# A hybrid SSD and gated-MLP layer on one core: a convolution on zero-padded copies, and the matmuls of an SSD group in fewer places

## Chip, cores and metric

The kernel runs on 1 core of one Trainium2 chip. The metric is the device time of one execution in microseconds. Five engines work side by side: PE (TensorE, matmuls), DVE (VectorE), ACT (ScalarE), POOL (GpSimd) and SP, which here only issues DMAs. Each engine takes its instructions strictly in the order in which the program holds them.

## The reference, cut to what matters

One layer: 256 context tokens and 256 latent tokens, width 2048. The normed and modulated tokens go through one input projection; its first 4096 columns (32 tiles of 128 channels) get a depthwise convolution of five taps and a SiLU, and feed a bidirectional Mamba-2 scan (SSD) in 8 groups of 4 heads and chunks of 128 tokens.

```python
def _dwconv_rows(x, w, b, n_rows, row_len):
    xp = pad(x.reshape(bsz, n_rows, row_len, C), 2 zeros on both ends of each row)
    y = b
    for k in range(5):
        y = y + xp[:, :, k:k + row_len] * w[k]
xbc = silu(_dwconv_rows(z[..., :4096], conv_w, conv_b, n_rows, row_len))
# context: 1 row of 256; latent: 4 rows of 64
states = einsum('bckgn,bckgr,bckgrp->bcgrpn', Bc, decay_to_end, xdt)
CB = einsum('bcqgn,bckgn->bcgqk', Cc, Bc)
y_diag = einsum('bcgqk,bcgrqk,bckgrp->bcqgrp', CB, exp(masked differences of cumsum(dt*A)), xdt)
y_off = einsum('bcqgn,bcgrpn,bcqgr->bcqgrp', Cc, h_starts, exp(acs))
out = x + gate * rmsnorm(concat(rmsnorm((y + D*x) * silu(z_ssd)), gated_mlp) @ w_out)
```

## The kernel before, in words

Every large product runs on PE as three matmuls of split operands (`mm3`, lines 139 to 141: high times high, high times low, low times high). For that, ACT casts each half of a streamed weight tile (`hi_w`, line 80) and DVE subtracts (`lo_w`, line 81), some halves ahead of PE, in four buffers.

The program has stages. First the adaLN products and seven of the 32 channel tiles are made, k by k, with their order written by hand. Then comes the stage that the change touches, about 137 to 480 us: the other 25 channel tiles are projected one after the other into a PSUM tile `psx` of a pool with two banks (`acp`), 48 matmuls a tile (512 columns, or 256 for the eight tiles of the C matrix, which only the latent tokens need). Between them the work of the SSD is strewn in. After it come 16 blocks of latent columns (`pa`, lines 877 to 879), the output projection (`pm`, `pq`), and a tail of norms and stores.

The order in the SSD stage comes from `later` and `pump`: `plan_tile` (line 660) files each step of a tile or a group under a due time, counted in units of which a tile takes 8 x 1.3 (8 x 0.65 for a C tile), and `pump` issues what is due after every second k step. A scheduler may move instructions a little within that. Group g consists of tiles 4g to 4g+3: two of x, one of B, one of C. Its steps:

- `conv_silu` (line 433): ACT writes `acc` = bias + middle tap (line 439), straight from the PSUM tile; DVE adds the four other taps (line 452), each as two instructions, one over the context row (252 to 255 columns) and one over the four latent rows (4 x 62 or 4 x 63), since a tap must not run over a row's end; ACT makes the SiLU (line 455). Tiles 4, 5 and 7 are first copied from PSUM to SBUF (`z4`, `z5`, `z7`, in unused parts of `y`).
- `ssd_x`, `ssd_b`: PE transposes x and B (`ptx`, `ptb`), ACT copies them out; `ssd_w`: POOL weighs x (`xw`, `xl`).
- `ssd_cb` (line 615): `pcb`, C times B for both chunks, on PE; DVE masks it (`cbf`, `cbb`).
- `ssd_states` (line 596): `psc` and `psl` on PE; ACT copies, POOL scales (line 612), DVE adds (line 613): the start states `hs`.
- `ssd_y(g, c)`, for one chunk: POOL starts `M` (line 633), DVE adds four heads (636) and multiplies by the decays `E` (638); PE makes `pso` = C times `hs` (640); DVE scales it into `yo`, POOL adds it to `y`.
- `ssd_yd(g, c)`: `psy` = `M` times x on PE (line 655), DVE adds it to `y`.
- `plan_e`: the decays of the next group. POOL issues a DMA of rows (`R`, line 529), ACT adds the columns (581), DVE takes the minimum (583, into `E`), ACT the exponential (590). `E`, `M`, `R` and `hs` have one buffer each, so that a new `M` waits until `psy` has read the old one, and `R` is loaded anew when `E` has been taken from it.

Of the kernel before, what the change touches and what calls it, by code (L numbers as in the profile page):

```python
# [40 lines left out]
def tile_hybrid_ssd_mlp(  # L41
# [388 lines left out]

    done = {}

    def conv_silu(i, src):
        ch = ORDER[i]
        lat = ch >= 24
        n = 256 if lat else 512
        acc = cv2.tile([P, n], F32, tag="acc", name=f"acc{i}")
# [4 lines left out]
        src4 = src[:, l0 : l0 + 256].rearrange("p (r t) -> p r t", r=4)
        for k in (0, 1, 3, 4):
            s = k - 2
            parts = [(acc4, src4, 64)]
            if not lat:
                parts.append((acc[:, 0:256], src[:, 0:256], 256))
            for (a, z, w) in parts:
                o0, o1 = max(0, -s), w - max(0, s)
                ao = a[..., o0:o1]  # L450
                zi = z[..., o0 + s : o1 + s]
# [1 line left out]
        tag = "xs" if ch < 16 else ("bs" if ch < 24 else "cs")
        o = cv2.tile([P, n], F32, tag=tag, name=f"xbc{i}")
        nc.scalar.activation(o, acc, AF.Silu)
        done[i] = o
# [171 lines left out]
    def ssd_y(g, c):  # L628
        S = gs_[g]
        E, cbf, cbb, xk, ct, hs = S["E"], S["cbf"], S["cbb"], S["xk"], done[4 * g + 3], S["hs"]  # L630
        h4 = slice(4 * g, 4 * g + 4)
# [7 lines left out]
        pso = spt([P, 2, 256], f"pso{g}{c}")  # L639
        nc.tensor.matmul(pso, lhsT=ct[:, c * P : (c + 1) * P], rhs=hs[:, c], start=True, stop=True)  # L640
        yo = cv1.tile([P, 2, 256], F32, tag="yo", name=f"yo{g}{c}")
        nc.vector.tensor_tensor(yo.rearrange("p d (h q) -> p d h q", h=4), pso.rearrange("p d (h q) -> p d h q", h=4),
                                bc(eac[:, c, :, h4], 3, 64), op=ALU.mult)
        yg = y[:, c, g * 256 : (g + 1) * 256]
        nc.gpsimd.tensor_tensor(hp(yg), hp(xk[:, 2 + c, :]), bc(dsk[:, h4], 2, 64), op=ALU.mult)
        nc.gpsimd.tensor_tensor(yg, yg, yo[:, 0, :], op=ALU.add)
        nc.gpsimd.tensor_tensor(yg, yg, yo[:, 1, :], op=ALU.add)
        S["M", c] = M

    def ssd_yd(g, c):  # L650
# [1 line left out]
        M, xk = S["M", c], S["xk"]
        psy = spt([P, 256], f"psy{g}{c}")
        for h in range(4):
            nc.tensor.matmul(psy[:, h * 64 : (h + 1) * 64], lhsT=M[:, h, :],
                             rhs=xk[:, 2 + c, h * 64 : (h + 1) * 64], start=True, stop=True)
        yg = y[:, c, g * 256 : (g + 1) * 256]
        nc.vector.tensor_tensor(yg, yg, psy, op=ALU.add)
# [409 lines left out]
```

## Time and profile before

| | |
|---|---|
| runs | 1009.81, 1009.97, 1011.67 us; median 1009.97 |
| the profiled execution's own time | 1012.65 us |
| its span, first to last instruction | 1010.9 us |
| granted TensorE clock over the span | 0.99 |
| PE, DVE, ACT, POOL busy | 981.3, 624.5, 493.1, 120.7 us |
| matmuls of the SSD stage between their casts: lines 139 to 141 | 400 each of 382, 366 and 369 ns (pipelined, so these overlap) |

A row of the profile gives an instruction group's line in the kernel, its engine, the tiles it writes and reads, how often, and its time. "Idle before" is the time in which the engine stood still just ahead of it, with the instruction whose end released it. A matmul of split operands with 512 columns starts every 0.227 us, one with 256 every 0.12 us, whatever the length shown for it.

### The profile page before, as it was taken

Reading aid. Unit: us, or ns where it says so; the run is one execution under the profiler, and the core shown is the slowest. Engines: PE = TensorE matmul, PEld = TensorE weight load, DVE = VectorE, ACT = ScalarE, POOL = GpSimd, SP = SyncE. Lnnn points to the kernel's source line nnn. Section 1 sums busy time; section 2 is a strip of 40 time slices with the busy share of each in tenths; the row PEclk is TensorE's granted clock in tenths of the full one; section 3 lists DMA queues with packets and bytes.
Section 4 is the critical chain, followed back from the end, with each engine's and each line's share of the span. In section 5 each row is a group of like instructions: output and inputs, shape, how many; then the busy total and the mean of one; then the engine's idle time right before and its main releaser. Section 6 shows DMA issues by size and latency. Waiting matters only on the chain.

```text
span 1010.9 us, 14117 instructions
## 1 busy us (share of the span) xinstructions
PE 981.3 (97%) x5600; PEld 797.0 (79%) x5600; DVE 624.5 (62%) x947; ACT 493.1 (49%) x762; POOL 120.7 (12%) x166
## 2 busy tenths in 40 slices
PE   6899999989999999999999999999999999999996
PEld 2788887767888888787888888877888888888885
DVE  3544478876575676766567767666655554445636
ACT  3433359754745636353545343455465564346522
POOL 1000003552224233223000000000000000000000
PEclk9899999999999999999999999999999999999998
DMA  9999654133332323323887777685455555556722
GB/s 355 417 419 419 269 195 170 42 131 120 125 125 84 125 107 118 110 84 133 326 306 277 282 272 281 248 323 175 166 193 182 189 186 181 194 205 218 281 87 84
DMA packets 31218, 207.28 MB, mean 205 GB/s; under 512 B 3696, under 2 KB 3840, under 8 KB 7472
## 3 DMA queue, kind: packets, MB, share of 16 engines
q1 hardware_dynamic: 28224, 192.44, 50.7%
q0 software_dynamic: 2208, 12.73, 3.7%
q10 hardware_dynamic: 720, 1.20, 0.3%
q8 instruction: 44, 0.72, 0.3%
q14 instruction: 22, 0.18, 0.1%
HBM read 204.20 MB, written 2.16 MB: 204 GB/s over the span
## 4 chain that ended last, share of the span: by engine, by line
PE 75%; DMA 8%; DVE 6%; ACT 4%; issue 3%; POOL 2%; DVEq 0%; SPq 0%; ACTq 0%; POOLq 0%
PE psx L139 8%; PE psx L140 8%; PE psx L141 8%; PE pa L877 8%; PE pa L878 8%; PE pa L879 8%; DMA gate<-in_wada_dram 6%; PE psada L214 3%; PE pm L922 3%; PE pm L923 3%; PE pm L924 3%; DVE lo_w L81 2%; PE pq L923 2%; PE pq L922 2%; PE pq L924 2%
## 5 line engine op out<-in xcount | busy, mean ns | idle before, releaser
L81 DVE TENSOR_TENSOR lo_w<-w,hi_w 128x1024 fp32r<-128x1024 f32 x234 | 286.5, 1231 | 199.3 <-ACT hi_w L80 195.9
L80 ACT CAST hi_w<-w 128x1024 fp32r<-128x1024 f32 x234 | 246.0, 1052 | 293.1 <-PE pa L879 141.8
L877 PE MATMUL pa<-hi_w,hhi 128*128 128x512 f32 x512 | 202.4, 395 | 0.0
L879 PE MATMUL pa<-hi_w,hlo 128*128 128x512 f32 x512 | 199.5, 390 | 0.0
L878 PE MATMUL pa<-lo_w,hhi 128*128 128x512 f32 x512 | 199.4, 390 | 0.0
L139 PE MATMUL psx<-hhi,hi_w 128*128 128x512 f32 (+1 forms) x400 | 152.7, 382 | 1.3 <-DVE acc L452 1.3
L141 PE MATMUL psx<-hhi,lo_w 128*128 128x512 f32 (+1 forms) x400 | 147.4, 369 | 0.0
L140 PE MATMUL psx<-hlo,hi_w 128*128 128x512 f32 (+1 forms) x400 | 146.5, 366 | 0.0
L877 PEld LDWEIGHTS pa<-hi_w,hhi 128*128 128x128 f32 x512 | 96.2, 188 | 20.5 <-issue 1.4
L879 PEld LDWEIGHTS pa<-hi_w,hlo 128*128 128x128 f32 x512 | 96.1, 188 | 20.3
L878 PEld LDWEIGHTS pa<-lo_w,hhi 128*128 128x128 f32 x512 | 96.3, 188 | 19.1 <-issue 0.2
L139 PEld LDWEIGHTS psx<-hhi,hi_w 128*128 128x128 f32 x400 | 75.8, 190 | 14.5 <-issue 3.5
L452 DVE SCALAR_TENSOR_TENSOR acc<-psx,pc,acc 128x248 f32<-128x248 f32 (+1 forms) x204 | 84.1, 469 | 3.1 <-ACT acc L439 2.4
L141 PEld LDWEIGHTS psx<-hhi,lo_w 128*128 128x128 f32 x400 | 75.7, 189 | 12.7 <-issue 0.5
L140 PEld LDWEIGHTS psx<-hlo,hi_w 128*128 128x128 f32 x400 | 75.7, 189 | 12.3 <-issue 1.4
L738 DVE SCALAR_TENSOR_TENSOR junk<-gate,cb 128x2048 bf16<-128x2048 f32 x16 | 36.7, 2292 | 30.5 <-DMA gate<-in_wada_dram 30.4
L922 PE MATMUL pm<-hi_w,hhi 128*128 128x512 f32 x128 | 50.0, 390 | 0.0
L923 PE MATMUL pm<-lo_w,hhi 128*128 128x512 f32 x128 | 49.9, 390 | 0.0
L924 PE MATMUL pm<-hi_w,hlo 128*128 128x512 f32 x128 | 49.7, 389 | 0.0
L581 ACT ACTIVATE R<-R,y 128x128 f32<-128x128 f32 x128 | 40.1, 390 | 14.6 <-DMA R<-acs 14.5
L139 PE MATMUL psx<-hhi,hi_st 128*128 128x512 f32 (+1 forms) x112 | 40.9, 365 | 0.0
L140 PE MATMUL psx<-hlo,hi_st 128*128 128x512 f32 (+1 forms) x112 | 40.8, 364 | 0.0
(217 smaller groups left out, 1270.5 us busy)
## 6 DMA issues: line engine op xcount, KB each, us to landing
w<-in_wlat_dram SPq DMA_DIRECT2D x64, 1024.0 KB, 4.8
ada<-in_wada_dram SPq DMA_DIRECT2D x32, 1024.0 KB, 14.5
w<-in_wout_dram SPq DMA_DIRECT2D x32, 1024.0 KB, 4.7
w<-in_wxbc_dram SPq DMA_DIRECT2D x25, 1024.0 KB, 4.8
gate<-in_wada_dram SPq DMA_DIRECT2D x16, 1024.0 KB, 5.7
R<-acs POOLq DMA_DIRECT2D x8, 1024.0 KB, 5.4
wst<-in_wst_dram SPq DMA_DIRECT2D x16, 480.0 KB, 13.8
xT<-in_xch_dram SPq DMA_DIRECT2D x4, 1024.0 KB, 10.0
```

The lines of the kernel that those rows point to most:

```text
L80: nc.scalar.copy(hi, raw)
L81: nc.vector.tensor_tensor(lo, raw, hi.bitcast(F32), op=ALU.subtract)
L139: nc.tensor.matmul(ps, lhsT=whi, rhs=hhi[k][:, s], start=start, stop=False)
L140: nc.tensor.matmul(ps, lhsT=whi, rhs=hlo[k][:, s], start=False, stop=False)
L141: nc.tensor.matmul(ps, lhsT=wlo, rhs=hhi[k][:, s], start=False, stop=stop)
L452: nc.vector.scalar_tensor_tensor(ao, zi, cw[:, k : k + 1], ao, op0=ALU.mult, op1=ALU.add)
L877: nc.tensor.matmul(pa[tk], lhsT=hhi[k][:, t], rhs=whi[:, w], start=k == 0, stop=False)
L878: nc.tensor.matmul(pa[tk], lhsT=hhi[k][:, t], rhs=wlo[:, w], start=False, stop=False)
L879: nc.tensor.matmul(pa[tk], lhsT=hlo[k][:, t], rhs=whi[:, w], start=False, stop=k == KT - 1)
L922: nc.tensor.matmul(p, lhsT=yh[:, t], rhs=whi[:, w], start=j == 0, stop=False)
L923: nc.tensor.matmul(p, lhsT=yh[:, t], rhs=wlo[:, w], start=False, stop=False)
L924: nc.tensor.matmul(p, lhsT=yl[:, t], rhs=whi[:, w], start=False, stop=hf == 0 and j == 15)
```

## The change

Convolution: a tile with context and latent tokens is first copied into an SBUF tile of 524 columns, with two zeros ahead of and behind the 256 context tokens and every row of 64 latent tokens; ACT does it, in two copies out of PSUM, into one of two such tiles (`zp`), whose zeros POOL has written once. `z4` and `z5` get that form too, by two DVE copies each. ACT's first tap and DVE's four others then run over 520 columns at once, one instruction a tap. The SiLU writes the two parts back without the gaps, as two instructions. C tiles are computed in place in the output tile, but else as before.

SSD group: `ssd_y` is split. `ssd_m` makes `M` and writes the product back over `E`, so that `psy` reads `E` and `M` is free at once. `ssd_o` makes `pso` of both chunks, one behind the other; `ssd_yd` makes `psy` of both. `ssd_cb` is due with `ssd_states`, both `pso` at 13 (they were at 9 and 12.5), both `psy` at 17.5 (13 and 17.5), the next group's decays from 18 (13). `gate`, `ssq` and `rr` move into one small tile, `at` to other columns of `y`.

```diff
+    def pad_rows(z, c0):
+        return z[:, c0 : c0 + 264].rearrange("p (r q) -> p r q", q=66)[:, :, 0:64]
+    def pad_in(copy, z, src):
+        copy(z[:, 2:258], src[:, 0:256])
+        copy(pad_rows(z, 260), src[:, 256:512].rearrange("p (r q) -> p r q", q=64))
...
+    nc.gpsimd.memset(y0[:, 384 : 384 + 2 * ZP], 0.0)
...
-                nc.vector.tensor_copy((z4, z5)[i], psx[4 + i])
+                pad_in(nc.vector.tensor_copy, (z4, z5)[i], psx[4 + i])
...
+    zps = [cv1.tile([P, ZP], F32, name=f"zp{n}") for n in range(2)]
...
-        nc.scalar.activation(acc, src, AF.Identity, bias=pc[:, C_CB + i : C_CB + i + 1], scale=cw[:, 2:3])
...
-                nc.vector.scalar_tensor_tensor(ao, zi, cw[:, k : k + 1], ao, op0=ALU.mult, op1=ALU.add)
...
+            pad_in(nc.scalar.copy, z, src)
+        n = ZP - 4
+        a = acc[:, 0:n]
+        nc.scalar.activation(a, z[:, 2 : 2 + n], AF.Identity, bias=cb, scale=cw[:, 2:3])
         for k in (0, 1, 3, 4):
+            nc.vector.scalar_tensor_tensor(a, z[:, k : k + n], cw[:, k : k + 1], a, op0=ALU.mult, op1=ALU.add)
+        nc.scalar.activation(o[:, 0:256], acc[:, 0:256], AF.Silu)
+        nc.scalar.activation(o[:, 256:512].rearrange("p (r q) -> p r q", q=64), pad_rows(acc, 258), AF.Silu)
...
-        nc.vector.tensor_tensor(M, M, E[:, c], op=ALU.mult)
+        nc.vector.tensor_tensor(E[:, c], M, E[:, c], op=ALU.mult)
...
+        pso = [spt([P, 2, 256], f"pso{g}{c}") for c in range(2)]
+        for c in range(2):
+            nc.tensor.matmul(pso[c], lhsT=ct[:, c * P : (c + 1) * P], rhs=hs[:, c], start=True, stop=True)
...
-            later(d0 + 5, lambda: ssd_cb(g))
+            later(d0 + 6, lambda: ssd_cb(g))
             later(d0 + 6, lambda: ssd_states(g))
-            later(d0 + 9, lambda: ssd_y(g, 0))
-            later(d0 + 12.5, lambda: ssd_y(g, 1))
-            later(d0 + 13, lambda: ssd_yd(g, 0))
-            later(d0 + 17.5, lambda: ssd_yd(g, 1))
-            plan_e(d0 + 13, g + 1)
+            later(d0 + 9, lambda: ssd_m(g, 0))
+            later(d0 + 12, lambda: ssd_m(g, 1))
+            later(d0 + 13, lambda: ssd_o(g))
+            later(d0 + 17.5, lambda: ssd_yd(g))
+            plan_e(d0 + 18, g + 1)
```

How instructions move shows in the order in which the engines hold them. On PE, in group 1, from `psl` (the second part of the states) to the first `pso`, before; the rows left out are matmuls of the projection, 30 of 256 columns and 2 of 512 in all:

```order
L606 MATMUL psl_2171<-xl_2103,bk_2000 128x256 x2
L139 MATMUL psx_2126<-hhi_125,hi_w_1896 128x256
...
L141 MATMUL psx_2126<-hhi_134,lo_w_1960 128x256
L139 MATMUL psx_2231<-hhi_119,hi_w_2045 128x512
L140 MATMUL psx_2231<-hlo_135,hi_w_2045 128x512
L640 MATMUL pso_2224<-hs_2174,xbc_1764 128x512
```

The same place of the changed kernel; 30 matmuls of 256 columns, 18 of 512 and the transposes of one B tile stand between:

```order
L632 MATMUL psl_2162<-xl_2067,bk_1992 128x256 x2
L141 MATMUL psx_2117<-hhi_124,hi_w_1889 128x256
...
L143 MATMUL psx_2215<-hhi_121,lo_w_2022 128x512
L593 MATMUL ptb_2240<-ident,xbc_2128 128x128 x4
...
L143 MATMUL psx_2215<-hhi_123,lo_w_2022 128x512
L672 MATMUL pso_2259<-hs_2165,xbc_1760 128x512
L672 MATMUL pso_2260<-hs_2165,xbc_1760 128x512
```

Both `pso` now stand together, 16 projection matmuls and a transpose further behind the states than the first did. From `psl` to the first `pso` there are, before and now, in groups 0 to 7: 29 and 30, 32 and 48, 18 and 36, 18 and 30, 12 and 30 (groups 4 to 6), 9 and 27 projection matmuls.

On POOL, from the first `M` of group 0 on, before, with what each waits for:

```order
L633 TENSOR_TENSOR M_1944<-cbb_1910,dtt 128x512 [waits DMAHW2_49,DVE_49]
L612 TENSOR_TENSOR hs_1925<-hs_1925,ed 128x256 [waits Activation_49] x2
L633 TENSOR_TENSOR M_2007<-cbb_1910,dtt 128x512 [waits DVE_49,PE_49]
L646 TENSOR_TENSOR y<-y,yo_1953 128x256 [waits DVE_49,Pool_49]
L647 TENSOR_TENSOR y<-y,yo_1953 128x256 [waits Pool_49]
L556 TENSOR_TENSOR xw_2098<-xk_1981,ed 128x256 [waits Activation_49]
```

And in the changed kernel:

```order
L659 TENSOR_TENSOR M_1937<-cbb_1909,dtt 128x512 [waits DMAHW2_49,DVE_49]
L638 TENSOR_TENSOR hs_1918<-hs_1918,ed 128x256 [waits Activation_49] x2
L659 TENSOR_TENSOR M_1985<-cbb_1909,dtt 128x512 [waits DVE_49,Pool_49]
L680 TENSOR_TENSOR y<-y,yo_2003 128x256 [waits DVE_49]
L681 TENSOR_TENSOR y<-y,yo_2003 128x256 [waits Pool_49]
L582 TENSOR_TENSOR xw_2062<-xk_1966,ed 128x256 [waits Activation_49]
```

The order is the same here, but the second `M` waits for DVE alone and no longer for PE.

## Rows read from the trace of the kernel before

**Rows 1.** The page, first part: each engine's busy time, share and instructions.
```profile
PE 981.3 (97%) x5600; PEld 797.0 (79%) x5600; DVE 624.5 (62%) x947; ACT 493.1 (49%) x762; POOL 120.7 (12%) x166
```

**Rows 2.** Windows of the SSD stage: us, then PE, PEld, DVE, ACT, POOL busy; PEclk, DMA, GB/s.
```profile
200.00:240.00 40.00, 35.18 (x162) 26.73 (x161) 28.36 (x57) 24.60 (x52) 18.37 (x25) 0.96 0.35 132
...
sum 340.00, PE 331.12 PEld 267.60 DVE 240.45 ACT 184.43 POOL 112.55; mean PE 41.39 PEld 33.45 DVE 30.06 ACT 23.05 POOL 14.07
```

**Rows 3.** Waits of PE over the span: us in total, how many, the longest.
```profile
PE pso L640 <- DVE hs L613: 5.2, 4, 2.2
...
PE psx L139 <- DVE acc L452: 1.3, 1, 1.3
...
PE ptb L567 <- ACT xbc L455: 0.7, 1, 0.7
PE pcb L620 <- ACT xbc L455: 0.7, 1, 0.7
...
PE ptx L547 <- ACT xbc L455: 0.5, 1, 0.5
PE psy L655 <- DVE M L638: 0.3, 1, 0.3
```

**Rows 4.** Timeline of PE, groups 0 and 1: start, length, instruction, idle before.
```profile
175.71 1.88 PE L603 MATMUL psc<-xw,bk 128*128 128x512 f32 x4
...
186.30 1.13 PE L640 MATMUL pso<-hs,xbc 128*128 128x512 f32 x2 [1.22 <-DVE hs L613]
...
199.35 1.88 PE L603 MATMUL psc<-xw,bk 128*128 128x512 f32 x4
...
209.90 1.99 PE L640 MATMUL pso<-hs,xbc 128*128 128x512 f32 x2 [2.19 <-DVE hs L613]
...
213.40 0.41 PE L139 MATMUL psx<-hhi,hi_w 128*128 128x512 f32 x1
```

**Rows 5.** Timeline of PE around pcb, psc and psl, in group 2 and in group 4.
```profile
230.00 0.39 PE L141 MATMUL psx<-hhi,lo_w 128*128 128x512 f32 x1
...
233.48 0.40 PE L140 MATMUL psx<-hlo,hi_w 128*128 128x512 f32 x1
...
317.51 0.39 PE L141 MATMUL psx<-hhi,lo_w 128*128 128x512 f32 x1
...
318.42 0.40 PE L140 MATMUL psx<-hlo,hi_w 128*128 128x512 f32 x1
...
319.33 0.39 PE L141 MATMUL psx<-hhi,lo_w 128*128 128x512 f32 x1
...
322.37 0.40 PE L140 MATMUL psx<-hlo,hi_w 128*128 128x512 f32 x1
```

**Rows 6.** Timeline of DVE: taps from PSUM (psx) and from SBUF (y), and hs.
```profile
155.76 6.29 DVE L452 SCALAR_TENSOR_TENSOR acc<-psx,pc,acc 128x248 f32<-128x248 f32 x16
...
163.10 0.83 DVE L452 SCALAR_TENSOR_TENSOR acc<-y,pc,acc 128x248 f32<-128x248 f32 x1
...
177.72 7.86 DVE L452 SCALAR_TENSOR_TENSOR acc<-y,pc,acc 128x248 f32<-128x248 f32 x16
185.50 0.74 DVE L613 TENSOR_TENSOR hs<-psl,hs 128x256 f32<-128x256 f32 x2
```

**Rows 7.** Timeline of POOL: xl beside the tap at 163.10, and group 0's two M.
```profile
163.62 2.34 POOL L559 TENSOR_TENSOR xl<-xk,ed 128x256 f32<-128x256 f32 x2
...
176.76 1.94 POOL L633 TENSOR_TENSOR M<-cbb,dtt 128x512 f32<-128x512 f32 x1 [6.05 <-DVE cbb L625]
...
190.33 1.04 POOL L633 TENSOR_TENSOR M<-cbb,dtt 128x512 f32<-128x512 f32 x1 [10.14 <-PE psy L655]
```

**Rows 8.** Groups of the same kind as the new instructions: busy and mean ns.
```profile
L975 DVE SCALAR_TENSOR_TENSOR xf<-og,ro,xf 128x512 f32<-128x512 f32 x8 | 5.6, 748 | 0.1
...
L608 ACT COPY hs<-psc 128x256 f32<-128x256 f32 x8 | 2.9, 367 | 10.6 <-PE psc L603 10.6
```

**Rows 9.** The page, last part: the row DMAs, KB each, us from issue to landing.
```profile
R<-acs POOLq DMA_DIRECT2D x8, 1024.0 KB, 5.4
```

More of the change, by code (lines that the diff above doesn't have):

```diff
@@ L29 @@
 WSSD = (0, 1, 2, 3, 4, 12, 5, 6, 13, 7, 8, 14, 9, 10, 15, 11)
+ZP = 2 + 256 + 2 + 4 * 66
 C_BADA, C_GPRE, C_GSSD, C_GMLP, C_BS, C_CW, C_CB, NPC = 0, 48, 64, 80, 96, 112, 272, 304
@@ L86, in tile_hybrid_ssd_mlp @@
     ypad = ctx.enter_context(mkpool(name="ypad", bufs=1, side="right"))
-    ypad.tile([P, 120], F32, name="ypad")
+    small = ypad.tile([P, 120], F32, name="small")
     ypool = ctx.enter_context(mkpool(name="ypool", bufs=1, side="right"))
@@ L129, in tile_hybrid_ssd_mlp @@
                                    op0=ALU.add, op1=ALU.mult)
-    gate = cpool.tile([P, 48], F32, name="gate")
+    gate = small[:, 0:48]
     nc.gpsimd.memset(gate, 0.0)
-    cpool.tile([P, 64], F32, name="cpad")
+    cpool.tile([P, 14], F32, name="cpad")
     hhi = [hpool.tile([P, TOK], F32R, name=f"hhi{k}") for k in range(KT)]
@@ L153, in yseg @@
         return y[:, j // 4, (j % 4) * 512 : (j % 4 + 1) * 512]
-    z4, z5, z7 = yseg(1), yseg(2), yseg(4)[:, 0:256]
+    y0 = y[:, 0]
+    z4, z5, z7 = y0[:, 384 : 384 + ZP], y0[:, 384 + ZP : 384 + 2 * ZP], yseg(4)[:, 0:256]
     zdt = yseg(3)
@@ L161, in tile_hybrid_ssd_mlp @@
     s2 = yseg(7)[:, 0:256]
-    at = y[:, 0, 256:512].rearrange("p (t h) -> p t h", t=4)
+    at = y0[:, 128:384].rearrange("p (t h) -> p t h", t=4)
     fold = yseg(7)[:, 256:320]
@@ L431, in tile_hybrid_ssd_mlp @@
     done = {}
+    zps = [cv1.tile([P, ZP], F32, name=f"zp{n}") for n in range(2)]
+    for z in zps:
+        nc.gpsimd.memset(z, 0.0)
+    zn = [0]
     def conv_silu(i, src):
@@ L435, in conv_silu @@
         lat = ch >= 24
-        n = 256 if lat else 512
-        acc = cv2.tile([P, n], F32, tag="acc", name=f"acc{i}")
         cw = pc[:, C_CW + 5 * i : C_CW + 5 * i + 5]
-        nc.scalar.activation(acc, src, AF.Identity, bias=pc[:, C_CB + i : C_CB + i + 1], scale=cw[:, 2:3])
-        l0 = 0 if lat else 256
-        acc4 = acc[:, l0 : l0 + 256].rearrange("p (r t) -> p r t", r=4)
-        src4 = src[:, l0 : l0 + 256].rearrange("p (r t) -> p r t", r=4)
-        for k in (0, 1, 3, 4):
[L444 to L451, printed above, removed]
-                nc.vector.scalar_tensor_tensor(ao, zi, cw[:, k : k + 1], ao, op0=ALU.mult, op1=ALU.add)
@@ L453, in conv_silu @@
[L453 to L456, printed above, removed]
+        cb = pc[:, C_CB + i : C_CB + i + 1]
+        o = cv2.tile([P, 256 if lat else 512], F32, tag="xs" if ch < 16 else ("cs" if lat else "bs"), name=f"xbc{i}")
+        done[i] = o
+        if lat:
+            nc.scalar.activation(o, src, AF.Identity, bias=cb, scale=cw[:, 2:3])
+            o4 = o.rearrange("p (r t) -> p r t", r=4)
+            src4 = src.rearrange("p (r t) -> p r t", r=4)
+            for k in (0, 1, 3, 4):
+                s = k - 2
+                o0, o1 = max(0, -s), 64 - max(0, s)
+                ao = o4[..., o0:o1]
+                nc.vector.scalar_tensor_tensor(ao, src4[..., o0 + s : o1 + s], cw[:, k : k + 1], ao,
+                                               op0=ALU.mult, op1=ALU.add)
+            nc.scalar.activation(o, o, AF.Silu)
+            return
@@ new lines, in conv_silu @@
+        if src is z4 or src is z5:
+            z = src
+        else:
+            z = zps[zn[0] % len(zps)]
+            zn[0] += 1
+            pad_in(nc.scalar.copy, z, src)
+        n = ZP - 4
+        acc = cv2.tile([P, ZP - 2], F32, tag="acc", name=f"acc{i}")
+        a = acc[:, 0:n]
+        nc.scalar.activation(a, z[:, 2 : 2 + n], AF.Identity, bias=cb, scale=cw[:, 2:3])
+        for k in (0, 1, 3, 4):
+            nc.vector.scalar_tensor_tensor(a, z[:, k : k + n], cw[:, k : k + 1], a, op0=ALU.mult, op1=ALU.add)
@@ L626, in ssd_cb, with ssd_m @@
         S["cbf"], S["cbb"] = cbf, cbb
-    def ssd_y(g, c):
+    def ssd_m(g, c):
         S = gs_[g]
-        E, cbf, cbb, xk, ct, hs = S["E"], S["cbf"], S["cbb"], S["xk"], done[4 * g + 3], S["hs"]
-        h4 = slice(4 * g, 4 * g + 4)
+        E, cbf, cbb = S["E"], S["cbf"], S["cbb"]
         M = cv1.tile([P, 4, P], F32, tag="M", name=f"M{g}{c}")
@@ L637, in ssd_y @@
                                            M[:, h, :], op0=ALU.mult, op1=ALU.add)
-        nc.vector.tensor_tensor(M, M, E[:, c], op=ALU.mult)
[L639 to L650, printed above, removed]
-        S = gs_[g]
[L652 to L658, printed above, removed]
+        nc.vector.tensor_tensor(E[:, c], M, E[:, c], op=ALU.mult)
@@ new lines, in ssd_o @@
+    def ssd_o(g):
+        S = gs_[g]
+        xk, ct, hs = S["xk"], done[4 * g + 3], S["hs"]
+        h4 = slice(4 * g, 4 * g + 4)
+        pso = [spt([P, 2, 256], f"pso{g}{c}") for c in range(2)]
+        for c in range(2):
+            nc.tensor.matmul(pso[c], lhsT=ct[:, c * P : (c + 1) * P], rhs=hs[:, c], start=True, stop=True)
+        for c in range(2):
+            yo = cv1.tile([P, 2, 256], F32, tag="yo", name=f"yo{g}{c}")
+            nc.vector.tensor_tensor(yo.rearrange("p d (h q) -> p d h q", h=4),
+                                    pso[c].rearrange("p d (h q) -> p d h q", h=4),
+                                    bc(eac[:, c, :, h4], 3, 64), op=ALU.mult)
+            yg = y[:, c, g * 256 : (g + 1) * 256]
+            nc.gpsimd.tensor_tensor(hp(yg), hp(xk[:, 2 + c, :]), bc(dsk[:, h4], 2, 64), op=ALU.mult)
+            nc.gpsimd.tensor_tensor(yg, yg, yo[:, 0, :], op=ALU.add)
+            nc.gpsimd.tensor_tensor(yg, yg, yo[:, 1, :], op=ALU.add)
@@ L660, in plan_tile, with ssd_yd @@
+    def ssd_yd(g):
+        S = gs_[g]
+        E, xk = S["E"], S["xk"]
+        for c in range(2):
+            psy = spt([P, 256], f"psy{g}{c}")
+            for h in range(4):
+                nc.tensor.matmul(psy[:, h * 64 : (h + 1) * 64], lhsT=E[:, c, h, :],
+                                 rhs=xk[:, 2 + c, h * 64 : (h + 1) * 64], start=True, stop=True)
+            yg = y[:, c, g * 256 : (g + 1) * 256]
+            nc.vector.tensor_tensor(yg, yg, psy, op=ALU.add)
     def plan_tile(i, src, d0=0.0, tx=7.0, tw=8.0, late=0.0):
@@ L706, in tile_hybrid_ssd_mlp @@
             plan_tile(7, z7, 6, late=21)
-    ssq = cpool.tile([P, 3, 2, 4], F32, name="ssq")
-    rr = cpool.tile([P, 3, 2], F32, name="rr")
+    ssq = small[:, 48:72].rearrange("p (i t j) -> p i t j", i=3, t=2)
+    rr = small[:, 72:78].rearrange("p (i t) -> p i t", i=3)
     def rms(i):
```

## The prediction, written before the changed kernel ran

> **What bounds the kernel.** I began with the page's busy times. PE is busy for 981.3 of the span's 1010.9 us, no other engine for more than 62% of it [rows 1]: PE sets the time, and a change pays only through what PE does or waits for. The windows from 140 to 480 us, the only stage touched, come next: PE is busy for 331.12 of 340 us, so it stands still for 8.88, and 4.82 of that lie between 200 and 240 us, where the granted clock is also at its lowest, 0.96 [rows 2]. Then PE's waits, which tell what it stood for: the start states `hs` ahead of `pso` 5.2 us in four waits, the conv's `acc` ahead of a projection matmul 1.3, ACT's SiLU ahead of `ptb`, `pcb` and `ptx` 0.7, 0.7 and 0.5, `M` ahead of `psy` 0.3 [rows 3]; together 8.7. The change leaves the count and shapes of PE's instructions in this stage as they are, and it doesn't touch what PE does after the stage. So the sum is about these waits, what follows them, and new ones.
>
> **Fewer places: nothing.** Whether a switch between the projection and a small product costs PE time is read around them. From the matmul ahead of a lone `pcb` to the second matmul behind it are 0.91 us; less two matmuls at 0.227 that is 0.45. The same for `psc` with `psl` is 3.04 - 0.455 = 2.585. In group 2 all three happened to stand together, and cost 3.48 - 0.455 = 3.03 [rows 5]: the sum of the two, so putting them together saves 0. I take `pso` and `psy` alike.
>
> **The waits for `hs` (-5.2).** `hs` is done about 10.5 us after `psc` starts, in group 0 (175.71 to 186.24, the end of DVE's sum) and in group 1 (199.35 to 209.90) [rows 4, 6]. What stands on PE between is now, in group 1: `psc` and `psl` 2.6, 30 matmuls of 256 columns at 0.12, 18 of 512 at 0.227 and four transposes at about 0.45 (as `pcb`'s): 10.7 us. In group 0 it is 2.6 + 30 x 0.227 + 0.9 = 10.3. Those two would just cover it even if `hs` came no sooner. It does come sooner in group 0, where it stood on DVE behind 16 taps on SBUF of 7.86 us [rows 6]: now 8 double-length taps at 0.748, that of the nearest instruction (same operation, 512 columns, SBUF) [rows 8], 6.0 us, 1.9 less. In the later groups the distance is 8.7 us or more; the four waits lie in groups 0, 1, 2 and 7, none in 3 to 6 with 12 to 18 matmuls between, where 30 stand now. I take all 5.2.
>
> **What followed the waits (-1.7, -1.0).** After group 1's wait PE ran its two `pso` and four projection matmuls in 3.50 us (209.90 to 213.40) [rows 4]; at full pace they are 0.87 + 4 x 0.227 = 1.77. The row falls from 0.63-us to 0.41-us matmuls there, and the granted clock is lowest in this window [rows 2]: the stop cost PE a stretch on the lower level, 1.2 in place of 2.4 GHz. That is 1.7 more for this wait. Behind the three others the same count gives 0.2 to 0.5 each, mostly a weight load laid bare; 1.0 in all.
>
> **The wait for `acc` (-1.3).** The PSUM bank of `psx` was free when ACT and eight DVE taps had read it. Now two ACT copies free it, 2 x 0.367 by the copy of `hs` (256 columns from PSUM) [rows 8]. PE fills the other bank in 48 x 0.227 = 10.9 us, so 0.7 us is covered unless ACT itself is late. ACT gets 22 such pairs, 16 us, and a second SiLU for 24 tiles, 24 x 0.37 = 9 at most, on 184 busy of 340 [rows 2]: 209, still under DVE's 240.
>
> **`M` (-0.3).** POOL's second `M` stood for `psy` 10.14 us in group 0 [rows 7], since `psy` read the only buffer. With the product in `E` it waits for DVE alone. POOL has 112.55 busy of 340, so `M` is early and PE's 0.3 goes.
>
> **DVE and POOL: nothing on the path.** A tile's four taps of 0.748 are 3.0 us; the eight short ones were 8 x 0.39 = 3.1 (16 in 6.29 us [rows 6]). Lower bound for the new tap: 0.39 x 2 less one start, some 0.6; upper: the 0.83 of a short tap from SBUF beside POOL's `xl` [rows 6, 7], doubled. The first would win DVE 0.15 x 4 a tile, hidden; the second is a rival. POOL's zeros are four fills ahead of the stage or at its start, cover its idle time.
>
> **New: the next group's decays (+0.7).** The rows `R` of the next group can be loaded only when `E` is free, now behind both `psy`, and `plan_e` is due at 18 in place of 13. The DMA needs 5.4 us from issue to landing [rows 9]; ACT then adds columns in strict order, and SiLU and the copies of `psx` stand behind those adds, `ptx` behind the SiLU. Nothing in the trace of before has this wait in full; bounds are 0 (the DMA lands before ACT has come there) and 1 to 1.6 a group. From distances on PE I get 0.1 to 0.5 in some groups; over five, in the lower part: 0.7. The waits for the SiLU, 1.9 together, I let stand.
>
> **Sum.** -5.2 - 1.7 - 1.0 - 1.3 - 0.3 + 0.7 = -8.8. The profiled execution took 1012.65, 2.7 above the runs' median, 1009.97; from the median the forecast is 1009.97 - 8.8 = **1001.2 us**, with 997 to 1005 as its own range (the new wait 0 to 3, the SiLU waits halved or grown, part of the 1.0 kept).
>
> **Rivals.**
> A, the waits form anew: the later `R` holds ACT in each of five groups by 1 to 1.6 us, of the size of the 1.3 and 1.2 seen [rows 3, 4], 5 to 8 in place of 0.7; with less elsewhere the gain is 2 to 6, so 1004 to 1008. For: ACT's order is strict, and the DMA's 5.4 us can't be shortened. Against: ACT keeps 340 - 209 = 131 us idle in this stage, and `ptx` is due late. 0.18.
>
> N, no change: `hs` turns out no earlier, other waits grow, and what is won at `pso` is lost at the SiLU, within 2 us, 0.2%, about what a measurement of this kernel tells from none: 1008 to 1012. That the change doesn't do what it says is excluded for `pso` and the second `M` by the order shown, not for the bank's release. 0.09.
>
> S, slower: the taps now read two SBUF inputs, `zp` and `acc`, where 22 tiles read one from PSUM, and POOL runs beside them. In the trace a tap from SBUF beside `xl` took 0.83 [rows 6, 7], against 0.49 for each of 16 others from SBUF [rows 6]. If each new tap is held for a whole POOL instruction, 1.04 to 1.94 for an `M` [rows 7], the four taps ahead of the sum of `hs` cost 4 to 8 us, and `hs` is late for `pso` though that stands further back; it decides from about 3.4 us of delay. In groups 0 to 3, where POOL is fullest, each wait then costs as group 1's did, 2.19 + 1.7 = 3.9: 15.6 in place of the 7.9 of now, +7.7; less 1.6 for `acc` and `M`: about 1016. The trace shows the 0.83 only, 0.34 more: 1.4 us for four taps, under 3.4. 0.12.
>
> The Trainium skill has a rule on this (page "SBUF — State Buffer", section "Who interferes with whom"): a DVE instruction with two SBUF inputs contends with a GpSimd one that reads SBUF, and the loser blocks for the whole of the other's instruction; with one SBUF input it doesn't contend. By that rule it would be S, 1016. The trace bears out the contention, not its size: the one plain pair was stretched by 0.34, less than the POOL instruction's 1.17 (2.34 for two).
>
> **How the numbers follow.** Forecast 0.61, A 0.18, N 0.09, S 0.12. The range reaches from a little under the forecast's low end, 996.5, to A's upper end, 1008; N and S above it and 0.05 below are left out, partly overlapped. Faster by over 0.2%: forecast and A, 0.79; within 0.2%: N, 0.09; slower: S, 0.12.
>
> **What would show it.** Right: in the profile after, no row of PE's waits for `hs` and none for `acc`; the granted clock 1.00 between 200 and 240 us; POOL's wait of `M` for `psy` gone; PE busy above 336 of the stage's 340 us; taps at 0.7 to 0.8. Each step wrong: a `pso` row with a wait above 0.5; taps above 1 us beside POOL (S); `ptx` or `ptb` waits that sum to 5 us behind ACT's adds to `R` (A); projection matmuls that wait for ACT's copies. The forecast as a whole is wrong if the PE idle time of the stage is still over 5 us, or if PE's own time there changes by over 2 us.

## The result, and the profile after

The changed kernel takes 1011.92 us (median of 20 runs, 1010.50 to 1016.19), the kernel before 1009.92 (20 runs, 1009.22 to 1011.67). The ratio is 1.0023, with a 95% interval of 1.0014 to 1.0031: slower by 2 us, where 8.8 us faster was forecast. Six of the 20 runs took 1013.6 to 1016.2 us, longer than any of the 20 of the kernel before.

The two profiled executions compare the wrong way: 1012.65 before, 1010.97 after. The first is 2.7 us above its median, the second 0.95 below. The verdict is the runs'; the profiles tell where the time lies. The one after is not of the six long runs, so no trace shows what those waited for.

The page's first part and the windows of the stage, after (columns as in [rows 1, 2]):

```profile
PE 979.6 (97%) x5600; PEld 797.7 (79%) x5600; DVE 619.2 (61%) x853; ACT 508.2 (50%) x830; POOL 137.4 (14%) x169
```
```profile
200.00:240.00 40.00, 34.43 (x164) 27.58 (x163) 27.95 (x48) 24.30 (x51) 18.86 (x24) 0.91 0.33 132
...
sum 340.00, PE 330.36 PEld 269.04 DVE 235.56 ACT 199.38 POOL 126.76; mean PE 41.30 PEld 33.63 DVE 29.45 ACT 24.92 POOL 15.84
```

PE stands still for 340 - 330.36 = 9.64 us, 5.57 of them between 200 and 240; before it was 8.88 and 4.82. The granted clock there is 0.91, not 1.00. POOL has 14.2 us more to show (126.76 against 112.55), with nearly the same instructions. PE's waits, after (us in total, how many, the longest):

```profile
PE ptb L593 <- ACT xbc L481: 7.7, 3, 5.6
...
PE ptx L573 <- ACT xbc L481: 1.8, 2, 1.1
```

Of [rows 3], `pso`, `acc`, `pcb` and `psy` are gone, and one wait of 5.6 us has come. It is in group 1, where the long `pso` wait had been, followed by matmuls of 0.63 us on the lower clock level (timeline of PE, after):

```profile
213.58 1.12 PE L593 MATMUL ptb<-ident,xbc 128*128 128x128 f32 x4 [5.57 <-ACT xbc L481]
214.35 0.78 PE L141 MATMUL psx<-hhi,hi_w 128*128 128x512 f32 x1
214.92 0.63 PE L142 MATMUL psx<-hlo,hi_w 128*128 128x512 f32 x1
```

`ptb` transposes the B tile of group 2, so it waits for that tile's SiLU. On ACT the SiLU stands behind additions to `R` and the load of a function table, and then waits 1.39 us for DVE's fourth tap (ACT, after):

```profile
210.44 1.28 ACT L481 ACT_TABLE_LOAD   x1
213.11 0.42 ACT L481 ACTIVATE xbc<-acc 128x256 f32<-128x256 f32 x1 [1.39 <-DVE acc L480]
```

The same SiLU in the kernel before, behind the first addition to `R` (ACT, before):

```profile
210.94 0.40 ACT L581 ACTIVATE R<-R,y 128x128 f32<-128x128 f32 x1 [7.17 <-DMA R<-acs]
...
212.65 0.63 ACT L455 ACTIVATE xbc<-acc 128x512 f32<-128x512 f32 x1
```

So the SiLU is only 0.46 us later than it was. But before, PE had stood in this group for 1.33 us at `acc` and 2.19 at `hs`, ran on the lower clock level behind that, and reached `ptb` at 214.80, without a wait. Now it is there at 208.01: much of what it no longer waits for earlier, it waits for here.

DVE there, after:

```profile
201.47 0.42 DVE L692 TENSOR_TENSOR y<-y,psy 128x256 f32<-128x256 f32 x1 [4.86 <-POOL y L681]
201.81 0.75 DVE L609 TENSOR_TENSOR E<-R 128x512 f32<-128x512 f32 x1
...
206.55 1.11 DVE L480 SCALAR_TENSOR_TENSOR acc<-zp,pc,acc 128x520 f32<-128x520 f32 x1
...
208.20 1.11 DVE L480 SCALAR_TENSOR_TENSOR acc<-zp,pc,acc 128x520 f32<-128x520 f32 x1
209.81 0.42 DVE L639 TENSOR_TENSOR hs<-psl,hs 128x256 f32<-128x256 f32 x1 [0.51 <-POOL hs L638]
210.16 0.75 DVE L480 SCALAR_TENSOR_TENSOR acc<-zp,pc,acc 128x520 f32<-128x520 f32 x1
211.99 0.42 DVE L639 TENSOR_TENSOR hs<-psl,hs 128x256 f32<-128x256 f32 x1 [1.08 <-POOL hs L638]
212.33 0.75 DVE L480 SCALAR_TENSOR_TENSOR acc<-zp,pc,acc 128x520 f32<-128x520 f32 x1
```

And POOL beside it:

```profile
205.87 2.88 POOL L582 TENSOR_TENSOR xw<-xk,ed 128x256 f32<-128x256 f32 x4
208.72 1.07 POOL L638 TENSOR_TENSOR hs<-hs,ed 128x256 f32<-128x256 f32 x1
209.74 1.64 POOL L585 TENSOR_TENSOR xl<-xk,ed 128x256 f32<-128x256 f32 x2
211.34 0.61 POOL L638 TENSOR_TENSOR hs<-hs,ed 128x256 f32<-128x256 f32 x1
```

The same eight instructions in the kernel before, beside taps from PSUM (POOL, before):

```profile
204.79 2.32 POOL L556 TENSOR_TENSOR xw<-xk,ed 128x256 f32<-128x256 f32 x4
207.07 1.17 POOL L559 TENSOR_TENSOR xl<-xk,ed 128x256 f32<-128x256 f32 x2
208.22 1.17 POOL L612 TENSOR_TENSOR hs<-hs,ed 128x256 f32<-128x256 f32 x2
```

Two things can be read here of DVE and POOL. DVE's add of the second `psy` waits 4.86 us for POOL, and the second minimum into `E` stands behind it, so the decays, and behind them ACT's copies of `psc` (at 204.27), are late. And taps of 0.75 us take 1.11, and an `hs` step of 0.61 on POOL takes 1.07, where the two engines are busy together; POOL's eight instructions take 6.1 us from the first `xw` to the last `hs`, before 4.6. Which of the two costs the time, the runs had to tell.

### The profile page after: what moved, and what is told of

The parts are those of the page before. It is cut to its first block, busy times and chain, and to the rows that moved or that the text cites. A ratio compares the mean times of both kernels' runs of the same rounds, so it can differ in the third digit from the quotient of the medians.

```text
span 1009.2 us, 14056 instructions
## 1 busy us (share of the span) xinstructions
PE 979.6 (97%) x5600; PEld 797.7 (79%) x5600; DVE 619.2 (61%) x853; ACT 508.2 (50%) x830; POOL 137.4 (14%) x169
## 4 chain that ended last, share of the span: by engine, by line
PE 86%; DVE 5%; ACT 4%; POOL 2%; DMA 2%; issue 1%; SPq 0%; DVEq 0%; ACTq 0%; POOLq 0%
PE pa L911 12%; PE pa L913 11%; PE pa L912 11%; PE psx L142 8%; PE psx L141 8%; PE psx L143 8%; PE psada L225 3%; PE pm L958 3%; PE pm L957 3%; PE pm L956 3%; PE pq L958 2%; PE pq L957 2%; PE pq L956 2%; DVE acc L480 2%; PE pso L672 1%
## 5 line engine op out<-in xcount | busy, mean ns | idle before, releaser
L83 DVE TENSOR_TENSOR lo_w<-w,hi_w 128x1024 fp32r<-128x1024 f32 x234 | 289.5, 1242 | 197.7 <-ACT hi_w L82 197.1
L142 PEld LDWEIGHTS psx<-hlo,hi_w 128*128 128x128 f32 x400 | 75.8, 190 | 12.5 <-issue 1.4
L480 DVE SCALAR_TENSOR_TENSOR acc<-zp,pc,acc 128x520 f32<-128x520 f32 x88 | 72.3, 826 | 5.5 <-ACT acc L478 4.7
```

Source lines behind the costliest of these rows:

```text
L83: nc.vector.tensor_tensor(lo, raw, hi.bitcast(F32), op=ALU.subtract)
L480: nc.vector.scalar_tensor_tensor(a, z[:, k : k + n], cw[:, k : k + 1], a, op0=ALU.mult, op1=ALU.add)
```

## The experiments

Two theories at first. **T1**: it is the order on DVE, the add ahead of the minimum. **T2**: taps with two SBUF inputs (`zp` and `acc`, where before one came from PSUM) and POOL's instructions hold each other up. T2 is called C from the second set of runs on. Each run stood beside runs of the kernel before on the same chip; "+" is slower than those by the medians.

**The convolution alone.** The changed kernel, with before's `ssd_y`, `ssd_yd` and due times.

```diff
-            later(d0 + 13, lambda: ssd_o(g))
...
+            later(d0 + 9, lambda: ssd_y(g, 0))
+            later(d0 + 12.5, lambda: ssd_y(g, 1))
...
+            plan_e(d0 + 13, g + 1)
```

> The new convolution with the SSD steps, buffers and due times of before. Theory T1 (order on DVE: in group 1 the add of the second psy stands ahead of the second minimum into E and waits 4.9 us for POOL, so the decays, ACT's copies of psc, POOL's and DVE's hs and, behind those, the conv's taps for the B tile come late, and ptb waits 5.6 us): the order of before is back, so no ptb wait above 2 us; the pso waits stay at 4 to 6 us, the acc wait is gone; 1007 to 1010 us. Theory T2 (taps with two SBUF inputs and POOL's instructions lengthen each other, and that alone eats the gain): POOL's busy time up by 12 us or more also here, pso waits grow above 6 us, 1011 to 1015 us.

1018.47 us, +7.9; ratio 1.0080 (1.0068 to 1.0092), and a `pso` wait of 6.3 us in group 1. T2's side, and more than it had expected, though POOL's busy time rose by 9.2 us (129.9 against 120.7), not 12. No tap of this profile took more than 1.42 us. The two engines slowed each other in many small steps: POOL's `xw`, `hs` and `xl` in group 1 took 6.7 us (205.30 to 211.98), and DVE's second `hs`, for which `pso` waited, ended at 212.43, before at 209.84.

**The SSD alone.** The kernel before with `ssd_m`, `ssd_o`, `ssd_yd` and the due times of the change.

```diff
-            later(d0 + 9, lambda: ssd_y(g, 0))
...
+            later(d0 + 9, lambda: ssd_m(g, 0))
+            later(d0 + 13, lambda: ssd_o(g))
...
+            plan_e(d0 + 18, g + 1)
```

> The SSD steps, buffers and due times of the change with the convolution of before (taps from PSUM, eight a tile). T1: the order of the adds and minima is that of the change, so ptb or ptx waits 3 to 6 us in group 1 in place of the pso waits: 1007 to 1012 us. T2: without the two-input taps the change pays: no pso wait, no wait above 2 us, POOL busy near 121 us, 1001 to 1004 us.

1007.88 us, -2.7; ratio 0.9971 (0.9960 to 0.9981). No `pso` wait. The time lies in T1's range, but with another wait than T1's, and T2's 1001 to 1004 us was missed. PE's waits of this run:

```profile
PE psx L139 <- DVE acc L452: 3.5, 2, 3.1
PE ptx L547 <- ACT xbc L455: 1.3, 1, 1.3
```

The stall of group 1 is now at PSUM's bank: the eight taps that free it come late, because DVE stands 4.28 us at the second `yo` (one buffer) until POOL has added the first (timeline of DVE, this run):

```profile
201.28 0.69 DVE L648 TENSOR_TENSOR yo<-pso,ed 128x512 f32<-128x512 f32 x1 [4.28 <-POOL y L654]
```

So the two halves of the change pull apart: the SSD gains, the convolution loses more.

**The adds behind the minima**, in the changed kernel:

```diff
+            S["psy", c] = psy
+    def ssd_ya(g):
...
             plan_e(d0 + 18, g + 1)
+            later(d0 + 21.5, lambda: ssd_ya(g))
```

> The changed kernel, with DVE's two adds of psy to y issued as a step of their own, due 3.5 later, so that in group 1 the second add stands behind both minima into E. T1: the chain E, exponential, copies of psc, hs, taps comes some 4 us earlier; the ptb wait falls from 5.6 to under 2 us and with it the half-clock stretch behind it: 1003 to 1007 us. T2: taps and POOL are as they were: the ptb wait stays above 4 us, 1010 to 1013 us.

1013.51 us, +2.9; ratio 1.0031 (1.0021 to 1.0041). The order is mended: both minima run at 195.98, and ACT copies `psc` at 200.97, 3.3 us earlier. Yet the `ptb` wait grew to 8.2, and the run is no faster: T1's forecast falls. DVE in group 1, this run:

```profile
205.76 4.94 DVE L662 SCALAR_TENSOR_TENSOR M<-cbf,dtt,M 128x128 f32<-128x128 f32 x2 [1.46 <-POOL M L659]
210.62 0.75 DVE L480 SCALAR_TENSOR_TENSOR acc<-zp,pc,acc 128x520 f32<-128x520 f32 x1
```

One step of `M` (two SBUF inputs, 0.35 us elsewhere) was held for 4.67 us and let go when POOL's unbroken run of `xw`, `hs` and `xl` (205.68 to 210.28) ended. The held instruction need not be a tap: DVE is in order, so what stands behind it, here all four taps, waits too.

But it is not this hold that `ptb` waited for. The last tap ended at 214.30, and the SiLU came 1.55 us later, behind eight additions to `R` and a table load; the DMA of `R` had kept ACT waiting (ACT, this run):

```profile
211.14 0.69 ACT L607 ACTIVATE R<-R,y 128x128 f32<-128x128 f32 x2 [9.55 <-DMA R<-acs]
...
215.85 0.42 ACT L481 ACTIVATE xbc<-acc 128x256 f32<-128x256 f32 x1
```

So this run refutes the early minimum as a cure, but does not show that held taps made its wait.

**`pso` later, alone**, in the kernel before:

```diff
+            later(d0 + 12, lambda: ssd_o(g, 0))
+            later(d0 + 13.2, lambda: ssd_o(g, 1))
```

> The kernel before with one edit: pso, its scaling and the adds to y of both chunks are steps of their own, due at 12 and 13.2 (pso stood behind M's steps, at 9 and 12.5); convolution, M, E and the decays as before. If the gain at pso that I had counted (5.2 of waits, 2.7 behind them) can be had by moving pso alone: pso waits under 1 us, 1002 to 1005 us. If the delay moves on to another wait whatever the rest does: some wait of 2 us or more takes its place in group 1, 1007 to 1011 us.

1013.42 us, +2.8; ratio 1.0031 (1.0019 to 1.0042): above both ranges. The `pso` waits are gone, and `ptb` 3.7, `ptx` 3.0 and `psy` 2.5 have come. A wait that is taken away at one place is won only if what follows on the other engines is not moved back with it.

**The kernel before, once more.**

> The kernel before, unchanged, for a second profile: the first one took 1012.65 us where its runs have a median of 1010. If the stalls on which I had counted are in every execution: about 1010 us, pso waits of 5.2 us again, 2.2 of them and a lower clock in group 1; the 2.7 us then lie elsewhere. If part of them was of that one execution: pso waits of 2.5 to 4 us and the clock at 1.00 between 200 and 240 us.

1011.42 us. `pso` 4.5 us (2.2 in group 1, clock 0.96), `acc` 1.4, `ptb` 0.3. The sum of PE in the stage is 332.21, idle 7.8, not 8.88. So the stalls are in both profiled executions of this kernel, and about 1.1 us of those on which I had counted were of the first one alone.

**Eight short taps, but from an SBUF copy**, and **the same copies, unused**. Both have the SSD of before:

```diff
+            nc.scalar.copy(z[:, 0:256], src[:, 0:256])
+            nc.scalar.copy(z[:, 256:512], src[:, 256:512])
+            src = z[:, 0:512]
```

The second run lacks the last line.

> The SSD of before, and the convolution of before but for its source: ACT copies each projected tile to SBUF (two copies, no gaps, no zeros), and the eight taps a tile read that copy in place of PSUM. Theory C (DVE instructions with two SBUF inputs and POOL's hold each other up, and this costs the new convolution its 8 us): as slow as the new convolution alone, 1014 to 1020 us, single taps of 0.8 us and more beside POOL, the pso wait of group 1 above 4 us. Theory D (it is the order: one long instruction a tap between M's and hs's steps, or ACT's extra work): 1008 to 1012 us, pso waits of 4 to 6 us.

> As the run with taps from an SBUF copy, with the same two ACT copies a tile, but the copy is not used: the taps read PSUM as before. C: the cost of the copies on ACT is hidden, 1009 to 1012 us, and the difference to the other run is 4 us or more. D, if ACT's extra work is the cause: as slow as the new convolution alone, 1014 to 1019 us.

With the taps from SBUF 1018.17 us (its profiled execution 1021.59, the longest of six), +6.9; ratio 1.0070 (1.0056 to 1.0084). With the copies alone 1011.72, +0.5; ratio 1.0007 (0.9998 to 1.0015). The two differ by one line: number and length of the taps are the same, and only the place of one input differs (of ACT's first tap too). That costs 6.5 us. It is theory C's time; its `pso` wait of over 4 us in group 1 did not come (3.0; `ptx`, `psy` and `ptb` waited 3.5, 2.4 and 1.7 in all). The taps of the first and of the second run (count: least, median, largest ns):

```profile
L474 DVE SCALAR_TENSOR_TENSOR acc<-zp,pc,acc x176: 461/474/5260, 143.1 to 459.1; 128x248 f32<-128x248 f32 x44, 128x254 f32<-128x254 f32 x44, 128x252 f32<-128x252 f32 x44, 128x255 f32<-128x255 f32 x44
```
```profile
L473 DVE SCALAR_TENSOR_TENSOR acc<-psx,pc,acc x204: 459/469/481, 142.7 to 455.7; 128x248 f32<-128x248 f32 x51, 128x252 f32<-128x252 f32 x51
```

The medians are alike; the largest is 5260 against 481. That one tap lies in group 1, DVE and POOL of the first run:

```profile
208.82 7.58 DVE L474 SCALAR_TENSOR_TENSOR acc<-zp,pc,acc 128x248 f32<-128x248 f32 x6
```
```profile
209.93 2.32 POOL L578 TENSOR_TENSOR xw<-xk,ed 128x256 f32<-128x256 f32 x4
212.22 1.18 POOL L581 TENSOR_TENSOR xl<-xk,ed 128x256 f32<-128x256 f32 x2
213.36 1.18 POOL L634 TENSOR_TENSOR hs<-hs,ed 128x256 f32<-128x256 f32 x2
```

POOL ran eight instructions without a gap for 4.6 us at its full pace, 0.58 to 0.59 each, and DVE stood at one tap meanwhile.

**POOL's run made shorter**: the run with taps from SBUF, with `xw` and `xl` computed by DVE.

```diff
-                nc.gpsimd.tensor_tensor(hp(xw[:, t, d, :]), hp(xk[:, t, :]), ...
+                nc.vector.tensor_tensor(hp(xw[:, t, d, :]), hp(xk[:, t, :]), ...
```

> The run with the eight short taps a tile from an SBUF copy (1018.2 us), and POOL's xw and xl, six multiplications a group, on DVE. DVE gets some 48 x 0.41 = 20 us more to do, POOL's unbroken run in group 1 (xw, xl, hs: 4.6 us, in which one tap took 5.26) is cut to hs alone. C: no tap above 2 us, and faster in spite of DVE's load, 1010 to 1015 us. If DVE's own load and order are what costs: slower, 1019 us or more.

1011.97 us, +0.5; ratio 1.0003 (0.9993 to 1.0013). DVE has more to do and the kernel is 6.4 us faster than with POOL's long run. (The kernel before did not run with this edit, so what a shorter queue on POOL is worth beside taps from PSUM is not shown.) No tap above 1.26 us:

```profile
L474 DVE SCALAR_TENSOR_TENSOR acc<-zp,pc,acc x176: 459/476/1260, 143.5 to 449.9; 128x248 f32<-128x248 f32 x44, 128x254 f32<-128x254 f32 x44, 128x252 f32<-128x252 f32 x44, 128x255 f32<-128x255 f32 x44
```

**The same edit in the changed kernel** (`xw` and `xl` on DVE).

> The changed kernel with one edit: POOL's xw and xl, six multiplications a group, run on DVE. DVE gets some 20 us more to do in the stage. C (in the changed kernel too, what eats the gain is that DVE's two-input instructions and POOL's runs hold each other): no tap above 1.2 us, the ptb wait of 5.6 us in group 1 under 2, faster than the changed kernel by 3 us or more, 1003 to 1009 us. If DVE's load and order are what costs: the waits move to psc or pso, 1012 us or more.

1007.81 us, -3.3; ratio 0.9967 (0.9955 to 0.9979). That is 5.3 us better than the changed kernel against its own reference runs (+2.0). The longest `ptb` wait is 2.7 in place of 5.6; under 2 was expected, and one tap still took 1.53. So in the changed kernel too POOL's `xw` and `xl` beside DVE's work are part of the loss. Which part of that work they hold up is not told apart: DVE's wait for POOL's adds, 4.86 us in the changed kernel, was 0.6 at most here, though the second minimum ended only 0.67 us earlier (201.89 against 202.56). The SiLU came at 210.58; it no longer waited for a tap, and four additions to `R` stood ahead of it in place of six.

**The SSD with its own waits mended**, the convolution of before: the SSD alone, `yo` in two buffers, and the adds behind the minima as above.

```diff
-            yo = cv1.tile([P, 2, 256], F32, tag="yo", name=f"yo{g}{c}")
+            yo = cv2.tile([P, 2, 256], F32, tag="yo", name=f"yo{g}{c}")
```

> The SSD of the change with the convolution of before, and two edits against the wait of DVE for POOL's adds (4.3 us in group 1 in the run with the SSD alone): yo has two buffers, and the adds of psy are a step of their own behind the minima into E. If that wait is what holds back psx's bank and the decays in group 1: the acc wait of PE (3.5 us) goes under 1 us, the clock stays at 1.00 between 200 and 220 us, 1001 to 1005 us. If the delay moves on to ptb or ptx as in the changed kernel with the adds moved: 1006 to 1010 us.

1005.04 us, -6.2; ratio 0.9943 (0.9931 to 0.9955): the fastest of all, faster than both kernels of the study. Its stage, by the same windows, and PE's waits in it:

```profile
200.00:240.00 40.00, 38.68 (x185) 30.25 (x184) 29.33 (x63) 26.43 (x55) 20.57 (x27) 1.00 0.36 132
...
sum 340.00, PE 335.18 PEld 272.78 DVE 241.27 ACT 188.33 POOL 114.86; mean PE 41.90 PEld 34.10 DVE 30.16 ACT 23.54 POOL 14.36
```
```profile
PE ptx L559 <- ACT xbc L467: 1.3, 1, 1.3
...
PE psx L141 <- DVE acc L464: 0.9, 1, 0.9
PE pso L658 <- DVE hs L625: 0.8, 1, 0.8
```

PE is idle for 4.8 us of the stage, and the clock stays at 1.00. Two edits were made at once; what each is worth alone was not run.

**The new convolution on top of that** (with one `zp` tile, since two and the second `yo` don't fit).

> The changed kernel with the two edits of the fastest run so far (two buffers for yo, the adds of psy behind the minima), and one zp tile in place of two, since there is no room for both. That run, with the convolution of before, took 1005.0 us. C (two-input taps are held by POOL's runs of instructions): the new convolution costs again what it cost before, 5 to 9 us more than that run, 1010 to 1014 us, with a ptb, ptx or pso wait of 4 us or more in group 1. If the new convolution only suffered from the order of the adds: 1003 to 1007 us.

1013.87 us, +2.4; ratio 1.0031 (1.0019 to 1.0043): 8.6 us more than the run without it, as C had expected. Not all of it need be held taps: there is one `zp` tile in place of two, and in group 1 six additions to `R` stood ahead of the SiLU on ACT, which ran 1.0 us after the last tap (216.52 against 215.51); in the run without the new convolution it ran ahead of them. Group 1 shows the tap that was held, 6.1 us of the three in this row (DVE, this run):

```profile
206.62 7.88 DVE L480 SCALAR_TENSOR_TENSOR acc<-zp,pc,acc 128x520 f32<-128x520 f32 x3
```

The single longest wait came out at 3.0, not 4 or more; the stalls are spread over groups 0 and 1 (PE busy 16.75 and 16.98 of 20 us from 180 to 200 and 200 to 220).

**One-operation taps for `z4` and `z5` alone**, on the fastest run:

```diff
+        if src is z4 or src is z5:
...
+            for k in (0, 1, 3, 4):
+                nc.vector.scalar_tensor_tensor(a, z[:, k : k + n], cw[:, k : k + 1], a, op0=ALU.mult, op1=ALU.add)
```

> The fastest run so far with the padded, one-operation taps for z4 and z5 alone, the two tiles that were in SBUF already; all other taps read PSUM. These two have two SBUF inputs either way, so C foresees no loss and DVE saves 8 short taps ahead of group 0's hs (some 1.5 us): 1003.5 to 1005.5 us. If the long taps as such cost (held or not): 1006 to 1009 us.

1008.90 us, -2.6; ratio 0.9977 (0.9965 to 0.9988): a miss, 3.6 us worse than the run without it, though no tap was held (the eight took at most 1.15). The profiled execution, 1011.53, is 2.6 us above the median. The steps fell into another order. In group 1 the SiLU now stands behind ACT's first addition to `R`, which waits for the DMA (ACT, this run):

```profile
209.70 0.40 ACT L608 ACTIVATE R<-R,y 128x128 f32<-128x128 f32 x1 [7.46 <-DMA R<-acs]
210.12 1.28 ACT L482 ACT_TABLE_LOAD   x1
211.42 0.63 ACT L482 ACTIVATE xbc<-acc 128x512 f32<-128x512 f32 x1
```

PE's `ptb` waits 3.3 us for it. In the fastest run that SiLU ran at 205.02, ahead of the addition to `R`. This is read from the trace; no run took that wait away by itself.

## Why the prediction was wrong, step by step

- **The step that failed, first**: "DVE and POOL: nothing on the path". The convolution was to give 1.3 us (the wait for `acc`). It costs 7.9 alone and 4.7 on top of the SSD's part (+2.0 against -2.7), and moving one input of the taps to SBUF costs 6.5 by itself. The tap was sized well (0.748 forecast, 0.757 median), and my upper price, 0.83 doubled, was not passed in the profiles of the changed kernel (1.53 at most) and of the convolution alone (1.42). What I had put at nothing is what such stretches add up to when DVE and POOL wait for each other's results: POOL's eight instructions in group 1 took 6.1 and 6.7 us in place of 4.6. In three other runs one instruction was held far longer, an `M` step for 4.67, taps for 5.26 and 6.14. Rival S named the contention and had it decide from 3.4 us of delay; it got 0.12, since the one pair that I had looked at lost 0.34. The convolution alone landed at 1018.5, near S's 1016, but through one place in group 1 mostly, not four, and with taps of 1.1 us, not each held for a whole POOL instruction: the nearness of the two numbers is in part luck.
- **The step that failed, second**: "The waits for the SiLU, 1.9 together, I let stand". They are 9.5 in the profile after (`ptb` 7.7, `ptx` 1.8). In group 1 the SiLU had been late before, at 212.65, and PE's own stops ahead of it had hidden that. I took their whole length as gain and did not ask what PE would meet next.
- **What I overlooked in the trace of before**: taps from SBUF and from PSUM have nearly the same mean there, but their largest tell them apart (the group of `acc` on DVE, kernel before):

```profile
L452 DVE SCALAR_TENSOR_TENSOR acc<-psx,pc,acc x204: 457/469/481, 142.4 to 455.8; 128x248 f32<-128x248 f32 x51, 128x252 f32<-128x252 f32 x51
L452 DVE SCALAR_TENSOR_TENSOR acc<-y,pc,acc x20: 461/472/1255, 163.1 to 185.1; 128x248 f32<-128x248 f32 x6, 128x252 f32<-128x252 f32 x6, 128x254 f32<-128x254 f32 x4, 128x255 f32<-128x255 f32 x4
```

  Of 204 taps from PSUM none lost anything beside POOL; of 20 from SBUF the worst took 2.7 times its length. It is the first of the 16 in [rows 6], at 177.72, beside POOL's `M` of 1.94; I had read that row by its mean, 0.49. In the changed kernel 100 of the 128 taps are of the second kind.
- **The rule that spoke against the change.** The Trainium skill, page "SBUF — State Buffer", section "Who interferes with whom", says that a DVE instruction with two SBUF inputs contends with a GpSimd one that reads SBUF, and that the one that comes second blocks until the other's instruction has ended. I set it aside on one pair. The runs bear it out, and three of them go further: the block of 5.26 us, for one, was longer than any one POOL instruction; it lasted about as long as POOL had the next instruction ready.
- **The `pso` waits, -5.2**: gone, as forecast. But the gain was not PE's to keep: moved alone it cost 2.8 us, and with the whole SSD change it brought 2.7, since POOL's adds of `yo` now stand behind `xw` and `xl` and hold DVE through the one `yo` buffer. That wait was not in my list. With it and the order of the adds mended, the SSD's part gave 6.2 of the 7.5 forecast for it (8.8 less the 1.3 of `acc`). About 1.1 us of the stalls counted was of the one profiled execution.
- **The clock, -1.7**: the mechanism was right, the sign not. The 5.6 us stop put PE back on the lower level: 0.91 from 200 to 240 us, not 1.00. In the fastest run the stop is gone, and it is 1.00.
- **The wait for `acc`, -1.3**: right, gone. With the SSD alone it had grown to 3.5, so the copies do free the bank early; by themselves, unused, they cost 0.5 us (interval -0.2 to 1.5).
- **`M`, -0.3**: right for PE. POOL's wait of `M` for `psy` (30.1 us) is gone, but 26.7 us of waits for the product in `E` replace it, since `M` still has one buffer.
- **Fewer places, 0**: right. From the matmul ahead of `pcb`, `psc` and `psl` to the second behind them it is 321.35 - 317.87 = 3.48 us in group 4, as in [rows 5]:

```profile
317.87 0.39 PE L143 MATMUL psx<-hhi,lo_w 128*128 128x512 f32 x1
...
321.35 0.40 PE L142 MATMUL psx<-hlo,hi_w 128*128 128x512 f32 x1
```

- **The later `R`, +0.7**: too small. In the changed kernel's profile ACT's additions to `R` and the table load ended at 211.72. With the tap ready at once `ptb` would still have waited about 4.2 of its 5.57 us (less 1.39, an estimate from the rows above). The additions began no later than before (207.61 against 210.94), but six stood ahead of the SiLU and not one. Rival A's order, the SiLU behind them, decided the `ptb` wait of 8.2 us with the adds behind the minima and that of 3.3 in the last run above.

What stays open: how much of the changed kernel's own `ptb` wait is the late minimum, how much the slowed taps and how much ACT's order. With the minimum early it was longer, with POOL's run cut it was half; the two were not undone together there, and no run changed the order on ACT alone.

## What to carry to other kernels

Count the SBUF inputs of a DVE instruction before moving its source out of PSUM: beside a busy POOL, eight short taps with one input in PSUM were faster here than four long ones with both in SBUF. Look at the largest duration of a group, not only its mean, and at how long POOL runs without a gap: in the worst cases here one DVE instruction stood about that long, and everything behind it on DVE with it. When a wait of PE is removed by moving work later, list what that work releases on the other engines' queues (single buffers above all), and what PE meets next and whether that is ready any earlier, before counting the gain.

## What the runs showed of the hardware that was not expected

A DVE instruction with two SBUF inputs stood for 5.26 us through eight POOL instructions that followed each other without a gap and lost nothing themselves (0.58 to 0.59 us each). At other places the two took turns: taps of 0.75 us at 1.11, POOL's `hs` of 0.61 at 1.07. In the changed kernel POOL's two steps that start `y` and add the first half of `yo` rose from 683 and 832 to 1083 and 1225 ns on average, together 12.7 us more of its 14.2 (the other steps' rises and falls nearly cancel); with the SSD change alone POOL's busy time was 122.5 us, so this came with the convolution. I had expected only this second kind, and no run tells when it is the one and when the other.
